# Attention of a hybrid block: q loaded once and copied up by ScalarE, both halves of a head in turn

## The chip, the cores and the metric

The kernel runs on one core of a Trainium2 chip. The metric is device time in microseconds of one execution; the times shown are three runs. The profile is of one further execution, taken by the hardware profiler. Engines are named as in the profile: PE (matrix multiply) with PEld (its weight loads), DVE (VectorE), ACT (ScalarE), POOL (GpSimd) and SP (SyncE, which issues all the DMAs here).

## The reference

One transformer block over 1024 tokens of width 1024 in float32. From the normed input come a gated delta-rule branch (4 heads of 128, in chunks of 64 tokens: the state chain) and an attention branch (8 heads of 64). Their outputs go through the output projection, a residual and a gated feed-forward layer (width 2816). The change touches the attention branch:

```python
DILATED_PATTERNS = ((128, 1), (512, 4), (2048, 16))
def dilated_attention(q, k, v, rel_bias):
    ...
    parts = [dilated_band(qh, kh, vh, rel_bias, win, dil) for win, dil in DILATED_PATTERNS]
    ...
    wts = jnp.exp(ms - jnp.max(ms, axis=0, keepdims=True))
    out = jnp.sum(wts[..., None] * nums, axis=0) / jnp.sum(wts * ss, axis=0)[..., None]
```

Each query sees the last 128 tokens, every 4th of the last 512 and every 16th of the last 2048, with a bias by distance and head, and the three parts share one softmax. A key that several patterns reach counts as often as they reach it.

## The kernel before

**Who sets the order.** The kernel is written as many Python generators ("strands"), each of which yields one operation or waits for an event or a buffer. While the program is built, `Weaver.run` picks the next operation by estimated start times (`Op.__init__` has a cost for each operation, `LAG` the delays between engines, and DMAs have an estimated landing) and by the strand's priority (a small number goes first). The result is one fixed order for each engine's queue; on the chip each engine goes through its own and waits on semaphores. The state chain has priority 0, loads 3, attention 5, the projections (`main`) and the output projection (`out_proj`) 9: on PE these last two fill what the others leave. All operations are recorded at one line, L273, so the views go by tile names.

**The stage.** From about 270 us on, four things share the engines: the last projections of the input (`pj`; in the order bq1, bk1, bq2, bk2, bq3, bk3 and then the gates, `ORDER`, line 48), the state chain (tiles `p`, `state`, `R`, `vn`, `o`), attention, and from about 500 us on the output projection (`pw`), which needs attention's results.

**Attention.** Keys and queries of a projection are stored to DRAM by `proj_qk` in two halves of 512 tokens, each as a high and a low part (`d_q`, `d_k`; `ev_q2[m][b]` and `ev_k2[m][b]` fire when half b of the pair of heads m is stored). Work goes by groups (z, hd): half z of the tokens of head hd. `a_order` (line 1446) lists the 16 groups: the first half of heads 0 to 3, the second of heads 0 and 1, the first of heads 4 to 7, then the second of heads 2 to 7. For each group in this order

- `head_loads` (line 1449) waits for both halves of q and k of its pair of heads, then issues the loads: `qs0` and `qs1` (q high and low, each loaded twice, to partitions 0 to 63 and 64 to 127), `ks` (k high on the lower and low on the upper partitions, 512 tokens for z = 0 and 1024 for z = 1) and `strip` (the biases). These tiles have two buffers each, so one group is loaded ahead;
- `head_prep` (line 1472) adds the parts to `qf` on DVE or POOL, whichever the planner finds earlier;
- `value_loads` (line 1480) loads values twice: `vn` (near keys, by classes of tokens, four DMAs of 32 partitions, 4 or 5 slots of 128) and `vf` (far keys, one or two blocks of four);
- `unit` (line 1499) is one tile of 128 queries, four for each group: score matmuls into `pS`, of `qs` against near keys and of `qf`, in four rows of 32, against far keys (the first tile of z = 0 has no far keys); bias and minimum on DVE (`Sr`, `mx`), exponential on ACT, transposes on PE (`tp`), and splits into high and low parts on ACT and DVE (`ptn`, `ptf`);
- `values` (line 1571) multiplies them by the values into `pV`, 12 matmuls for z = 0 and 18 for z = 1, adds the parts on ACT and DVE (`plow`, `ptmp`) and stores to `d_mix`.

`attention` (line 1607) starts a unit when at most FLY = 6 others are under way.

**Behind it.** `mix_load` (line 1694) loads token tile t of the result when all eight heads have finished half t // 4 of the tokens, so `out_proj` can begin its first tile when the first half is done for every head. Loading the weights of the output projection (`load_wo`: `wor`, `woh`, `wol`) starts after the state chain. The loads of the feed-forward weights (`wraw`) start when attention is done.

Of the kernel before, what the change touches and what calls it, by code (L numbers as in the profile page):

```python
# [11 lines left out]
F32 = mybir.dt.float32  # L12
F32R = mybir.dt.float32r
# [8 lines left out]
P = 128  # L22
S = 1024
# [4 lines left out]
AH = 8  # L28
# [13 lines left out]
TAIL = 5  # L42
ATT = 700.0
EARLY = 4
PWO = (2, 3, 2)
SWITCH = 120.0
BREATH = 200.0
# [3 lines left out]
def sub(ap, dims, off=0):  # L51
    return bass.AP(tensor=ap.tensor, offset=ap.offset + off, ap=[list(d) for d in dims])
# [475 lines left out]
def block_kernel(ctx: ExitStack, tc: tile.TileContext, a, out):  # L528
# [888 lines left out]
    def chain_out(o, t):  # L1417
# [14 lines left out]
        for c in range(2):  # L1432
# [10 lines left out]
    ev_lv = {key: Event() for key in ev_ld}  # L1443
    ev_att = [[Event() for _ in range(4)] for _ in range(AH)]

    a_order = [(0, 0), (0, 1), (0, 2), (0, 3), (1, 0), (1, 1), (0, 4), (0, 5), (0, 6), (0, 7),
               (1, 2), (1, 3), (1, 4), (1, 5), (1, 6), (1, 7)]

    def head_loads():
        for z, hd in a_order:  # L1450
            n = 512 * (z + 1)
            c0 = S - n
            m, e = hd // 2, hd % 2
            r0 = hd * 64
            for b in range(2):
                yield ev_q2[m][b]
                yield ev_k2[m][b]

            qs = []
            for i in range(2):  # L1460
                z_ = yield at.get([P, 512], F32R, name="qs%d" % i)
                for x in (0, 64):
                    yield SY.dma_start(z_[x:x + 64, :].bitcast(F32), d_q[m, i, 64 * e:64 * e + 64, c0:c0 + 512])
                qs.append(z_)
            ks = yield at.get([P, S], F32R, name="ks")
            for i in range(2):
                yield SY.dma_start(ks[64 * i:64 * i + 64, 0:n].bitcast(F32), d_k[i, r0:r0 + 64, 0:n])
            strip = yield at.get([P, 576], F32, name="strip")
            yield SY.dma_start(strip[:], d_bias[hd])
            w.spawn(head_prep(z, hd, qs, ks, strip, c0), 3)  # L1470

    def head_prep(z, hd, qs, ks, strip, c0):

        qf = yield at.get([P, 512], F32, name="qf")
        yield After(*[q[:] for q in qs])
        yield Either(*[x.tensor_tensor(qf[:], qs[0][:].bitcast(F32), qs[1][:].bitcast(F32), ALU.add) for x in (V, G)])
        cur[z, hd] = qs, qf, ks, strip, c0
        ev_ld[z, hd].fire()

    def value_loads():  # L1480
        for z, hd in a_order:
            for t in range(4 * z + 4):
                yield ev_v[hd // 4][t]

            k0 = 1 - z
            v = yield at.get([P, 5, P], F32R, name="vn")
            x = AH * P
            for r in range(4):
                yield SY.dma_start(v[32 * r:32 * r + 32, k0:, :].bitcast(F32),
                                   sub(d_v[:], [[4 * x, 32], [P * x, 5 - k0], [1, P]], hd * P + (3 * z * P + r) * x))  # L1490
            vf = []
            for b in range(z + 1):
                y = yield at.get([P, 4, P], F32R, name="vf", bufs=3)
                vf.append(y)
                yield SY.dma_start(y[:].bitcast(F32), sub(d_v[:], [[4 * x, P], [x, 4], [1, P]], hd * P + 512 * b * x))
            vals[z, hd] = v, vf
            ev_lv[z, hd].fire()

    def unit(z, hd, I, group):
# [34 lines left out]
        banks.put(ps)  # L1534
        n_sc[z, hd] = n_sc.get((z, hd), 0) + 1
        if n_sc[z, hd] == 4:
            at.put(*qs, qf, ks, strip)
        if len(parts) == 2:
            yield V.tensor_tensor(mx[:, 0:1], mx[:, 0:1], mx[:, 1:2], ALU.min)
        yield A.activation(Sr[:, 0:W], Sr[:, 0:W], AF.Exp, scale=-1.0, bias=mx[:, 0:1],  # L1540
# [29 lines left out]

    def values(z, hd, pts):
        yield ev_lv[z, hd]
        v, vf = vals[z, hd]
        m, e = hd // 2, hd % 2
        pn, far = pts
        yield After(pn[:], *[x[:] for x in far])
# [1 line left out]
        for h in range(2):  # L1578

            po = yield banks.get([P, 2, 4, 2, 32], F32, name="pV")  # L1580
            ops = []
            for k in (1, 3, 2, 4) + ((0,) if z else ()):
                i, n = (max(k - 1, 0), 2 if 0 < k < 4 else 1)
                ops.append((po[:, :, i:i + n].rearrange("p c i r j -> p c i (r j)"), v[:, k, :],
                            pn[:, :, max(2 * k - 1, 0):min(2 * k + 1, 8), 64 * h:64 * h + 64]))
            for k, f in enumerate(far):
                i = int(k == z)
                for r in range(2):
                    ops.append((po[:, :, i:, r, :], vf[k][:, 3 - 2 * h - r, :], f[:, :, 2 * h + r, i:, :]))
            yield [mm(o, l, r, n == 0, n == len(ops) - 1) for n, (o, l, r) in enumerate(ops)]  # L1590
            if not h:
                tmp = yield at.get([64, 512], F32, name="ptmp")
            low = yield at.get([64, 4, 2, 32], F32, name="plow", bufs=1)
            yield A.copy(low[:], po[0:64, 1])
            yield V.tensor_tensor(low[:], po[0:64, 0], low[:], ALU.add)

            tt = sub(tmp[:], [list(tmp[:].ap[0]), [P, 4], [-1, 2], [-4, 32]], 127 - 2 * h)
            yield V.tensor_tensor(tt, po[64:128, 0], low[:], ALU.add)
            banks.put(po)
            at.put(low)  # L1600
        at.put(v, *vf, pn, *far)
        yield SY.dma_start(d_mix[4 + m, 64 * e:64 * e + 64, z * 512:(z + 1) * 512], tmp[:])
        at.put(tmp)
        for g_ in range(2):
# [787 lines left out]
```

## Time and profile before

| | |
|---|---|
| three runs | 1271.48, 1273.46, 1274.88 us (median 1273.46) |
| the profiled execution | 1270.66 us, span 1268.9 us |
| mean granted PE clock | 0.997 |
| DMA bytes, mean rate | 216.40 MB, 171 GB/s over the span |
| attention: first and last score matmul | 290.4 and 528.7 us |
| attention: last value matmul | 550.5 us |

In the prediction, a row of a table of stretches has the start and end in us, the length, then for PE, PEld, DVE, ACT and POOL the busy time with the number of instructions, then PE's granted clock, the share of time in which the DMA engines were busy, and GB/s (fewer columns where the view is of one tile). A row of waits reads: engine and what waited, after the arrow what ended the wait, then the sum in us, the number of times, and the longest. A row of the chain has start, length and what it was; "DMA ks<-d_k" there is the time from issue to landing. A row of groups has the count, busy us, the mean ns of one, and the idle time ahead of it with what ended it. A row of DMA issues has the count and the KB of each.

### The profile page before, as it was taken

The numbers are of one execution on the slowest core, as the hardware profiler recorded it, in microseconds if no ns is written. First come the engines' busy times: TensorE is split into PE (matmuls) and PEld (weight loads), VectorE is DVE, ScalarE is ACT, GpSimd is POOL, SyncE is SP. The second block draws the span as 40 slices with busy tenths as digits, with TensorE's granted clock in tenths as the row PEclk, the third lists the DMA queues.
The fourth block names the chain that finished last, engine by engine and source line by source line (L and its number), as shares of the span: only waits on it lengthen the run. The fifth ranks groups of instructions, "written<-read, shape, count | busy, mean of one in ns | idle before, by whom it ended". The sixth has DMA issues, their size and how long they took to land.

```text
span 1268.9 us, 20103 instructions
## 1 busy us (share of the span) xinstructions
PE 1242.0 (98%) x6989; PEld 1026.7 (81%) x6989; DVE 974.3 (77%) x1913; ACT 562.9 (44%) x1162; POOL 180.1 (14%) x153
## 2 busy tenths in 40 slices
PE   8999999999999999999999999999999999999997
PEld 7888798788888787788788888888888887888886
DVE  5689969738988777867798878776677766975886
ACT  7544521136655556545554333333333334534541
POOL 1133411102221110100111101110001100000111
PEclk9999999999999999999999999999999999999999
DMA  8626463779985789667533543223333138734335
GB/s 281 209 73 181 147 206 104 143 228 288 280 232 179 216 251 260 203 217 231 191 125 119 167 155 108 86 77 104 125 125 102 42 106 311 253 128 151 97 124 199
DMA packets 177317, 216.40 MB, mean 171 GB/s; under 512 B 38032, under 2 KB 93712, under 8 KB 177216
## 3 DMA queue, kind: packets, MB, share of 16 engines
q1 hardware_dynamic: 177216, 215.12, 54.2%
q8 instruction: 56, 0.92, 0.3%
q14 instruction: 45, 0.37, 0.1%
HBM read 152.90 MB, written 64.52 MB: 171 GB/s over the span
## 4 chain that ended last, share of the span: by engine, by line
PE 60%; DVE 4%; DMA 4%; SPq 1%; issue 1%; ACT 1%; POOL 0%; DVEq 0%; POOLq 0%; ACTq 0%
PE bank L273 46%; PE pw L273 6%; PE pj L273 2%; PE tp L273 2%; PE p L273 1%; PE pV L273 1%; PE pS L273 1%; SPq L273 1%; DMA da<-d_hid 1%; DMA h2l<-d_h 1%; DMA wor<-in_w_out 1%; PE rp L273 1%; DMA ks<-d_k 0%; DMA qs<-d_q 0%; DVE x L273 0%
## 5 line engine op out<-in xcount | busy, mean ns | idle before, releaser
L273 PE MATMUL pj<-hTh,w 128*128 128x512 f32 x768 | 263.3, 402 | 5.6 <-ACT hTh L273 5.6
L273 PEld LDWEIGHTS pj<-hTh,w 128*128 128x128 f32 x768 | 145.5, 189 | 37.6 <-ACT hTh L273 5.6
L273 ACT CAST wbh<-wraw 128x512 fp32r<-128x512 f32 x130 | 80.2, 621 | 200.6 <-PE bank L273 129.0
L273 PE MATMUL pj<-hTl,w 128*128 128x512 f32 x384 | 151.0, 393 | 0.0
L273 DVE TENSOR_TENSOR wbl<-wraw,wbh 128x512 fp32r<-128x512 f32 x131 | 93.6, 717 | 30.0 <-ACT wbh L273 29.9
L273 PE MATMUL bank<-views 128*128 128x512 f32 (+1 forms) x307 | 85.6, 387 | 0.6 <-ACT views L273 0.6
L273 PEld LDWEIGHTS pj<-hTl,w 128*128 128x128 f32 x384 | 72.9, 190 | 12.4 <-DVE hTl L273 0.5
L273 PE MATMUL bank<-views,dah 128*128 128x512 f32 (+1 forms) x214 | 74.4, 384 | 0.0
L273 PE MATMUL bank<-dbh,views 128*128 128x512 f32 (+1 forms) x201 | 71.0, 383 | 0.0
L273 PEld LDWEIGHTS bank<-views 128*128 128x128 f32 x307 | 57.4, 188 | 13.1 <-ACT views L273 1.0
L273 POOL TENSOR_TENSOR m<-m,m 128x512 f32<-128x512 f32 x18 | 28.4, 1579 | 254.0 <-DVE r L273 168.6
L273 PE MATMUL pw<-woh,mh 128*128 128x512 f32 x128 | 51.9, 406 | 0.0
L273 PE MATMUL pw<-woh,ml 128*128 128x512 f32 x128 | 50.2, 392 | 0.0
L273 PE MATMUL pw<-wol,mh 128*128 128x512 f32 x128 | 50.1, 392 | 0.0
L273 PE MATMUL bank<-dbh,dah 128*128 128x512 f32 (+1 forms) x129 | 49.7, 386 | 0.0
L273 DVE SCALAR_TENSOR_TENSOR yc<-raw,convw,yc 128x1024 f32<-128x1024 f32 x36 | 47.1, 1308 | 0.3
L273 ACT CAST w<-wr 128x512 fp32r<-128x512 f32 x53 | 32.5, 619 | 32.7 <-PE pj L273 25.7
L273 ACT ACTIVATE Sr<-Sr,mx 128x512 f32<-128x512 f32 (+2 forms) x64 | 39.9, 624 | 15.5 <-DVE mx L273 15.0
L273 PEld LDWEIGHTS bank<-views,dah 128*128 128x128 f32 x214 | 39.9, 188 | 8.3
L273 DVE TENSOR_TENSOR m<-bank,m 128x512 f32<-128x512 f32 x44 | 30.1, 685 | 19.1 <-PE bank L273 19.1
L273 PEld LDWEIGHTS bank<-dbh,views 128*128 128x128 f32 x201 | 37.6, 188 | 8.3
L273 DVE TENSOR_TENSOR w<-wr,w 128x512 fp32r<-128x512 f32 x41 | 31.6, 781 | 15.2 <-ACT w L273 14.9
(387 smaller groups left out, 3288.3 us busy)
## 6 DMA issues: line engine op xcount, KB each, us to landing
wr<-in_w_in SPq DMA_DIRECT2D x56, 256.0 KB
wraw<-in_w_gate SPq DMA_DIRECT2D x52, 256.0 KB
wraw<-in_w_up SPq DMA_DIRECT2D x52, 256.0 KB
views<-d_hid SPq DMA_DIRECT2D x47, 256.0 KB
db<-in_w_down SPq DMA_DIRECT2D x40, 256.0 KB
qs<-d_q SPq DMA_DIRECT2D x64, 128.0 KB
da<-d_hid SPq DMA_DIRECT2D x30, 256.0 KB
vf<-d_v SPq DMA_DIRECT2D x24, 256.0 KB
```

The source lines that it names most:

```text
L273: op.fn(*op.args, **op.kw)
```

## The change

`a_order` takes both halves of heads 0 to 4 in turn, then the first half of heads 6, 7 and 5, then the second half of heads 5, 6 and 7. A group waits for half z of q and k only. q is loaded once, to the lower partitions; two ACT copies in `head_prep` fill the upper ones. For heads 0 to 5 (`once`) the second group keeps the first one's `ks` and `strip` and loads only the upper 512 keys. Values are loaded in blocks of 512 tokens, `vn` like `vf` with four slots and `VB` = 3 buffers each; for heads 0 to 5 the second group keeps the first one's block. The buffers are given back after the second group. `values` reads the same slots from the blocks.

```diff
+VB = 3
...
-    a_order = [(0, 0), (0, 1), (0, 2), (0, 3), (1, 0), (1, 1), (0, 4), (0, 5), (0, 6), (0, 7),
-               (1, 2), (1, 3), (1, 4), (1, 5), (1, 6), (1, 7)]
+    a_order = [(z, hd) for hd in range(5) for z in range(2)] + [(0, 6), (0, 7), (0, 5), (1, 5), (1, 6), (1, 7)]
+
+    once = range(6)
 
     def head_loads():
+        kept = {}
         for z, hd in a_order:
-            n = 512 * (z + 1)
-            c0 = S - n
+            c0 = (1 - z) * 512
             m, e = hd // 2, hd % 2
             r0 = hd * 64
-            for b in range(2):
-                yield ev_q2[m][b]
-                yield ev_k2[m][b]
 
             qs = []
+            yield ev_q2[m][z]
             for i in range(2):
                 z_ = yield at.get([P, 512], F32R, name="qs%d" % i)
-                for x in (0, 64):
-                    yield SY.dma_start(z_[x:x + 64, :].bitcast(F32), d_q[m, i, 64 * e:64 * e + 64, c0:c0 + 512])
+                yield SY.dma_start(z_[0:64, :].bitcast(F32), d_q[m, i, 64 * e:64 * e + 64, c0:c0 + 512])
                 qs.append(z_)
-            ks = yield at.get([P, S], F32R, name="ks")
+            yield ev_k2[m][z]
+            more = hd in kept
+            ks, strip = kept.pop(hd) if more else (None, None)
+            if not more:
+                ks = yield at.get([P, S], F32R, name="ks")
+            x, y = 512 if more else 0, 512 * z + 512
             for i in range(2):
-                yield SY.dma_start(ks[64 * i:64 * i + 64, 0:n].bitcast(F32), d_k[i, r0:r0 + 64, 0:n])
-            strip = yield at.get([P, 576], F32, name="strip")
-            yield SY.dma_start(strip[:], d_bias[hd])
+                yield SY.dma_start(ks[64 * i:64 * i + 64, x:y].bitcast(F32), d_k[i, r0:r0 + 64, x:y])
+            if not more:
+                strip = yield at.get([P, 576], F32, name="strip")
+                yield SY.dma_start(strip[:], d_bias[hd])
+                if hd in once:
+                    kept[hd] = ks, strip
             w.spawn(head_prep(z, hd, qs, ks, strip, c0), 3)
 
     def head_prep(z, hd, qs, ks, strip, c0):
+        for q in qs:
+            yield After(q[:])
+            yield A.copy(q[64:128, :], q[0:64, :])
 
         qf = yield at.get([P, 512], F32, name="qf")
-        yield After(*[q[:] for q in qs])
...
     def value_loads():
+        x = AH * P
         for z, hd in a_order:
-            for t in range(4 * z + 4):
-                yield ev_v[hd // 4][t]
-
-            k0 = 1 - z
-            v = yield at.get([P, 5, P], F32R, name="vn")
-            x = AH * P
-            for r in range(4):
-                yield SY.dma_start(v[32 * r:32 * r + 32, k0:, :].bitcast(F32),
-                                   sub(d_v[:], [[4 * x, 32], [P * x, 5 - k0], [1, P]], hd * P + (3 * z * P + r) * x))
-            vf = []
-            for b in range(z + 1):
-                y = yield at.get([P, 4, P], F32R, name="vf", bufs=3)
-                vf.append(y)
-                yield SY.dma_start(y[:].bitcast(F32), sub(d_v[:], [[4 * x, P], [x, 4], [1, P]], hd * P + 512 * b * x))
-            vals[z, hd] = v, vf
+            vals[z, hd] = vals.get((0, hd), [])[:1] if hd in once else []
+            for b in range(len(vals[z, hd]), z + 1):
+                for t in range(4 * b, 4 * b + 4):
+                    yield ev_v[hd // 4][t]
+
+                v = yield at.get([P, 4, P], F32R, name="vn", bufs=VB)
+                for r in range(4):
+                    yield SY.dma_start(v[32 * r:32 * r + 32].bitcast(F32),
+                                       sub(d_v[:], [[4 * x, 32], [P * x, 4], [1, P]], hd * P + (4 * b * P + r) * x))
+                vf = yield at.get([P, 4, P], F32R, name="vf", bufs=VB)
+                yield SY.dma_start(vf[:].bitcast(F32), sub(d_v[:], [[4 * x, P], [x, 4], [1, P]], hd * P + 512 * b * x))
+                vals[z, hd].append((v, vf))
             ev_lv[z, hd].fire()
...
-            at.put(*qs, qf, ks, strip)
+            at.put(*qs, qf, *(() if z == 0 and hd in once else (ks, strip)))
...
-                ops.append((po[:, :, i:i + n].rearrange("p c i r j -> p c i (r j)"), v[:, k, :],
+                ops.append((po[:, :, i:i + n].rearrange("p c i r j -> p c i (r j)"), blocks[z if k else 0][0][:, (k - 1) % 4, :],
...
-        at.put(v, *vf, pn, *far)
+        at.put(pn, *far)
+        if z or hd not in once:
+            for x in blocks:
+                at.put(*x)
```

More of the change, by code (lines that the diff above doesn't have):

```diff
@@ L1572, in values @@
         yield ev_lv[z, hd]
-        v, vf = vals[z, hd]
+        blocks = vals[z, hd]
         m, e = hd // 2, hd % 2
@@ L1588, in values @@
                 for r in range(2):
-                    ops.append((po[:, :, i:, r, :], vf[k][:, 3 - 2 * h - r, :], f[:, :, 2 * h + r, i:, :]))
+                    ops.append((po[:, :, i:, r, :], blocks[k][1][:, 3 - 2 * h - r, :], f[:, :, 2 * h + r, i:, :]))
             yield [mm(o, l, r, n == 0, n == len(ops) - 1) for n, (o, l, r) in enumerate(ops)]
```

## The prediction

> **What bounds the kernel now.** I read the page first, then the table of stretches over the part that the change touches (268 to 640 us), then the waits, the chain and the queue inside it. The page's head says which engine matters:
>
> ```profile
> span 1268.9 us, 20103 instructions
> PE 1242.0 (98%) x6989; PEld 1026.7 (81%) x6989; DVE 974.3 (77%) x1913; ACT 562.9 (44%) x1162; POOL 180.1 (14%) x153
> ```
>
> PE is busy for 98% of the span. The edit takes no matrix multiply away and adds none (see the value blocks below), so it can only give back or lose PE's idle time and PE's slow clock. How much of that lies in its reach, by stretch (start and end, length, then busy us of each engine with its instructions in brackets, PE's granted clock, DMA share, GB/s):
>
> ```profile
> 268.00:360.00 92.00, 89.27 (x678) 75.12 (x676) 74.36 (x233) 52.12 (x146) 18.84 (x19) 1.00 0.91 272
> 360.00:404.00 44.00, 42.83 (x324) 37.05 (x324) 37.84 (x113) 26.77 (x81) 10.51 (x9) 1.00 0.62 188
> 404.00:432.00 28.00, 24.66 (x197) 20.47 (x196) 19.79 (x76) 13.82 (x44) 3.67 (x3) 0.94 0.89 256
> 268.00:640.00 372.00, 361.31 (x2486) 299.63 (x2485) 291.41 (x799) 211.50 (x551) 58.77 (x59) 1.00 0.76 230
> ```
>
> PE idles 372.00 - 361.31 = 10.69 us in the whole part. One stretch is out of line: 404 to 432 loses 28.00 - 24.66 = 3.34 us, and its clock is 0.94, another 0.06 x 28 = 1.7 us. No gain far above 10.69 + 1.7 = 12.4 us can come out of this part. Why that stretch stalls is in three views: PE's and VectorE's waits in it, the chain, and SyncE's queue.
>
> ```profile
> PE pS L273 <- DMA ks<-d_k: 3.3, 2, 2.3
> ```
> ```profile
> DVE qf L273 <- DMA qs<-d_q: 5.5, 3, 4.4
> ```
> ```profile
> 415.24 6.25 DMA ks<-d_k
> ...
> 421.69 0.48 PE pS L273 x2
> ```
> ```profile
> 360.01 2.41 SPq L273 DMA_DIRECT2D qs<-d_q  x4
> ...
> 380.07 0.34 SPq L273 DMA_DIRECT2D d_k<-bh  x1
> ...
> 403.13 0.39 SPq L273 DMA_DIRECT2D d_k<-bh  x1
> ...
> 404.85 2.42 SPq L273 DMA_DIRECT2D qs<-d_q  x4
> ```
>
> The scores (pS) wait for keys that SyncE had issued by 415.24 and that landed 6.25 us later. Between 362.4 and 404.85 SyncE issued no q at all: the ninth group of the list, (0, 6), may not load before both halves of the last key projection are stored (403.13), and the list is served in order. Then the loads of several groups go out in a burst. The scores themselves show the hole (length, PE's busy time on pS, count in brackets, clock, DMA):
>
> ```profile
> 268.00:390.00 122.00, 22.46 (x272) 1.00 0.86 258
> 390.00:410.00 20.00, 0.00 (x0) 1.00 0.58 165
> 410.00:430.00 20.00, 6.69 (x84) 0.91 0.94 263
> ```
> ```profile
> L273 PE MATMUL pS<-ks,qs x128: 222/282/454, 290.7 to 527.8; 128*128 128x256 f32 x112, 128*128 128x128 f32 x16
> L273 PE MATMUL pV<-ptf,vf x96: 252/278/336, 305.9 to 550.5; 128*128 128x192 f32 x64, 128*128 128x256 f32 x32
> L273 PE MATMUL pj<-hTh,w x768: 387/389/793, 5.6 to 503.3; 128*128 128x512 f32 x192
> ```
>
> A first-half group has 32 recorded score matmuls and a second-half group 40 (a unit has two on q, and eight on qf where it has far keys), 576 in all. The 272 up to 390 are exactly the first eight groups (6 x 32 + 2 x 40); then none is left to do. PE bridges 390 to 410 with projections (pj), so the hole costs nothing there; it costs where attention restarts.
>
> **The change part by part.** *Order and gates.* The new list has ten groups (heads 0 to 4, both halves: 5 x 32 + 5 x 40 = 360 matmuls) ahead of head 6. At the pace before the hole, 272 in the 99 us from 290.7 to 390, or 2.7 per us, they last until 291 + 133 = 424; and (0, 6) now waits only for the first half of its projections, whose keys were stored at 380.07 instead of 403.13. Attention then takes PE time that the projections have here from 390 to 410, so that store comes later than 380, but 40 us are there for it. I take the hole as gone. What is late next is the ordinary idling around it: (2.73 + 1.17) us in the 136 us up to 404, so 0.8 in 28. The stretch gives 3.34 - 0.8 = 2.5 us of idling and 1.7 us of clock: **-4.2 us**. The ends: 0, if the restart only moves, and -5.0, if the stretch becomes free of gaps.
>
> *Fewer transfers.* From the page's list of DMA issues:
>
> ```profile
> qs<-d_q SPq DMA_DIRECT2D x64, 128.0 KB
> vf<-d_v SPq DMA_DIRECT2D x24, 256.0 KB
> strip<-d_bias SPq DMA_DIRECT2D x16, 288.0 KB
> ks<-d_k SPq DMA_DIRECT2D x16, 256.0 KB
> vn<-d_v SPq DMA_DIRECT2D x32, 80.0 KB
> ks<-d_k SPq DMA_DIRECT2D x16, 128.0 KB
> vn<-d_v SPq DMA_DIRECT2D x32, 64.0 KB
> ```
>
> These are 200 issues and 29,696 KB. After: qs 32; ks 28 of 128 KB and 4 of 256; strip 10; vf 18; vn 72 of 64 KB (blocks of four instead of strips of four or five): 164 issues and 20,800 KB. SyncE's queue is spared 36 issues, some 22 us at 2.42/4 each, and the DMA engines 30% of attention's bytes. Beside a busy PE that is worth nothing; it pays where a load is waited for. Such places are two waits of PE in the first stretch,
>
> ```profile
> PE pS L273 <- DMA d_k<-bh: 0.9, 1, 0.9
> PE pS L273 <- DMA ks<-d_k: 0.8, 1, 0.8
> ```
>
> and the gaps after q of (1, 6), which goes out behind the weights of the output projection (one row of the chain, then 10-us stretches):
>
> ```profile
> 475.60 5.41 DMA qs<-d_q
> ```
> ```profile
> 480.00:490.00 10.00, 9.64 (x56) 7.99 (x54) 8.74 (x17) 8.01 (x14) 1.29 (x1) 1.00 1.11 242
> 490.00:500.00 10.00, 8.90 (x72) 6.72 (x73) 7.87 (x28) 6.31 (x18) 0.00 (x0) 1.00 0.93 302
> ```
>
> I take half of each: **-0.8** of 1.7 and **-0.7** of 0.36 + 1.10. The ends are none and all.
>
> *An earlier end of attention.* The 304 scores after the hole took the 117 us from 411 to 528, 2.6 per us; at that pace, without the hole, 576 last 221 us and end near 512 instead of 528. The loads of the feed-forward weights start only when attention is done, and the stage behind them is short of VectorE time (18.98 of 20 us):
>
> ```profile
> 555.46 1.39 SPq L273 DMA_DIRECT2D wraw<-in_w_gate  x1
> ```
> ```profile
> 620.00:640.00 20.00, 18.55 (x86) 14.96 (x85) 18.98 (x32) 12.90 (x26) 4.93 (x4) 1.00 0.63 210
> ```
>
> Loads some 15 us sooner spread that preparation; of its 1.45 us of PE gaps I take **-0.5** (ends 0 and -1.45).
>
> *The copies.* 2 x 16 = 32 new copies of 64x512 on ScalarE, from the lower to the upper partitions. The trace has no such copy. The nearest rows:
>
> ```profile
> L273 ACT CAST bh<-bl 128x512 fp32r<-128x512 f32 x10 | 6.2, 621 | 13.8 <-DVE bl L273 11.2 <-POOL w L273 1.0 <-POOL state L273 0.8
> L273 ACT COPY vn<-p 64x512 f32<-64x512 f32 x15 | 8.7, 579 | 2.0 <-PE p L273 1.8
> ```
> ```profile
> L273 DVE TENSOR_TENSOR ptmp<-pV,plow 64x256 f32<-64x256 f32 x32 | 20.3, 636 | 1.0
> L273 DVE TENSOR_TENSOR plow<-pV,plow 64x256 f32<-64x256 f32 x32 | 13.2, 411 | 8.8 <-ACT plow L273 8.6
> ```
>
> As a plain copy 0.58 to 0.62 us. The only row with a move across the halves is VectorE's ptmp, which also reverses and strides: 636/411 = 1.55 times plow, so at most 0.96. I take 0.62, the row that also reads and writes SBUF: 32 x 0.62 = 19.8 us of ScalarE (ends 18.5 and 31). ScalarE is busy 211.5 of the 372 us, so there is room. The cover of the 1.24 us that they add to a group's load is the prefetch of one group, 32/2.7 = 12 us of scores. With the cover gone, and at the rate that the second rival works out, 10 us would reach PE. PE's waits on ScalarE are tenths of a us today; the only one of 360 to 404 is
>
> ```profile
> PE p L273 <- ACT vn L273: 0.2, 1, 0.2
> ```
>
> A tenth more work on ScalarE makes little of that; I take **+0.7** (ends 0 and +10).
>
> *The value blocks.* 8 x 12 + 8 x 18 = 240 value matmuls as before, with three buffers of each kind of block. A second-half group's new block waits until the group before it has given one back, a group ahead of its use: I take nothing; without that cover it costs one block's load, five issues or 3 us of queue, in part beside other PE work.
>
> Sum: -4.2 - 0.8 - 0.7 - 0.5 + 0.7 = **-5.5 us**. The profiled execution took 1270.66 us around its span of 1268.9, so it would take 1265.2. The median of the three runs shown, 1273.46, lies 2.8 above it; its counterpart is 1268.0.
>
> **The rivals.** *The room closes again* (chance 0.22). PE is busy for 97% of this part, its order is planned by estimates, and a new list moves every gap. Then the 404 stretch's loss comes back at another restart, the copies eat the small gains, and the time is 1273 (1270 to 1277). Against it: the hole has a cause that the new list takes away.
>
> *ScalarE becomes the gate* (0.19, slower). Today only VectorE or GpSimd stands still when q is late. After the edit ScalarE's queue holds a copy that waits for the DMA, and behind it stand the state chain's vn and o, the exponentials and the splits of ptn and ptf, which PE waits for. The price: in the stall above VectorE's longest wait of 4.4 us came with a PE wait of 2.3, a rate of 0.52. The waits for q in the whole part are
>
> ```profile
>   DMA qs<-d_q: 9.5, 7
> ```
>
> If these 9.5 us and the copies' 19.8 reach PE at that rate, it is 0.52 x 29.3 = +15.2; with the gains of 6.2 left, +9.0: 1282. It decides from a rate of 6.2/29.3 = 0.21 upwards. For it: landing times were missed by microseconds at 415. Against it: 30% of the bytes go. The Trainium skill says in "TensorE: Matmul & The Clock Gate", section "Architectural detail: the array is 16× 32×32, not 1× 128×128", that ScalarE and VectorE take their work strictly first in, first out. By that rule a late q stops all of ScalarE for the whole wait, which is this rival; the trace of before has such a wait on VectorE and, since ScalarE reads no q there, cannot show one on ScalarE.
>
> *The output projection starves* (0.07, slower). Its first attention tile needs the first half of all heads, and head 5's is now the 13th group of 16 instead of the eighth. Its 456th score comes at 291 + 456/2.7 or /2.6, 460 to 466, and its values some 23 us later (527.8 to 550.5 at the end of attention): by 489, ahead of 503.3, where the projections run out. With attention 15% slower it comes at 515, and PE, left with little but attention, loses most of 12 us: 1281 with the other terms as forecast less the restart's gain.
>
> **How the numbers follow.** Forecast 0.52, no change 0.22, ScalarE 0.19, starvation 0.07. A difference under 0.3% (3.8 us: 1269.6 to 1277.3) can't be told from none. The forecast's own range is 1264 (every gain at its full end, -9.6) to 1271 (half of the restart and little else); 0.06 of its 0.52 lies above 1269.6, and 0.02 of the second case below: faster 0.48, same 0.06 + 0.20 = 0.26, slower 0.19 + 0.07 = 0.26. The range goes from 1262, all of the 12 us, to 1281 and leaves out the upper halves of the two slow cases, 0.13, and little else.
>
> **What would show it.** Right: no 20 us without pS between 291 and the end of attention, clock 1.00 from 400 to 440, the last value matmul near 535, the first wraw near 540, copies of 0.6 us with ScalarE waiting less than 5 us for q. Wrong: waits of several us of ScalarE for q with PE waiting for vn, ptn or ptf behind them; a gap between the last pj and the first pw; a 3 us stall at another restart.

## The result, and the profile after

The changed kernel takes 1278.39 us (median of 10 runs, 1276.87 to 1283.94) where the kernel before takes 1272.24 beside it (10 runs, 1270.55 to 1275.72): a ratio of 1.0053 (95%: 1.0036 to 1.0071), 6 us slower. The forecast was 5.5 us faster. The profiled execution of the changed kernel took 1283.94 us, the longest of the ten; 2.6 us of its delay are there before attention starts, where the two kernels are the same. It is not a typical run: its mean granted clock was 0.994, and five of the ten had 0.997. What follows therefore goes by stretches, not by the span. Line numbers of the changed kernel are one higher (L274).

The page's head:

```profile
span 1282.2 us, 20077 instructions
PE 1251.6 (98%) x6989; PEld 1027.8 (80%) x6989; DVE 978.3 (76%) x1925; ACT 571.6 (45%) x1180; POOL 176.2 (14%) x151
```

PE's busy time grew by 9.6 us with the same 6989 matrix multiplies: part of the loss sits in multiplies that ran slowly, not in gaps. The table of stretches of the changed kernel, columns as before:

```profile
268.00:360.00 92.00, 88.81 (x681) 73.56 (x680) 71.22 (x218) 56.47 (x150) 15.09 (x16) 1.00 0.75 230
360.00:404.00 44.00, 42.20 (x338) 34.28 (x337) 39.28 (x126) 29.57 (x84) 11.29 (x10) 1.00 0.72 207
404.00:432.00 28.00, 26.86 (x227) 22.63 (x226) 25.17 (x82) 20.50 (x60) 7.96 (x7) 1.00 0.69 203
470.00:500.00 30.00, 26.83 (x190) 21.01 (x189) 20.04 (x61) 14.06 (x44) 1.27 (x1) 0.89 0.65 193
530.00:560.00 30.00, 26.28 (x140) 19.08 (x138) 14.13 (x26) 11.00 (x21) 1.12 (x2) 0.94 0.75 236
268.00:640.00 372.00, 358.30 (x2458) 291.26 (x2458) 282.04 (x787) 211.76 (x552) 49.31 (x53) 0.99 0.66 201
```

The old stall is gone, as forecast: 404 to 432 idles 1.14 us instead of 3.34, at clock 1.00 instead of 0.94. Two new ones stand in its place: 470 to 500 idles 3.17 us at 0.89, and 530 to 560 idles 3.72 us at 0.94. In the kernel before the same two stretches are these:

```profile
470.00:500.00 30.00, 28.54 (x186) 22.74 (x187) 20.01 (x54) 17.25 (x39) 1.29 (x1) 1.00 1.03 287
530.00:560.00 30.00, 29.48 (x186) 24.78 (x185) 20.84 (x53) 14.26 (x37) 1.91 (x3) 1.00 0.44 139
```

From the two tables, idle time changes by -2.2 at the old stall and by +1.7 and +3.2 at the new ones. The clock returns 0.06 x 28 = 1.7 us and takes 0.11 x 30 + 0.06 x 30 = 5.1.

That is not the whole difference of this pair of executions, which lie 13.3 us apart. To see the rest, the same work has to be compared, and not the same stretch of time: from the last multiply ahead of this stage (tile `pm`) to the first of the feed-forward layer (tile `bank`). The kernel before, the changed kernel, and further down `e5_gains_later`, which has neither stall:

```profile
267.40:621.10 353.70, 344.47 (x2410) 286.06 (x2408) 273.11 (x768) 199.58 (x527) 53.84 (x55) 1.00 0.77 232
270.00:636.00 366.00, 352.30 (x2408) 286.18 (x2409) 278.11 (x781) 209.07 (x546) 49.31 (x53) 0.99 0.66 199
268.10:623.60 355.50, 347.76 (x2410) 283.34 (x2408) 277.80 (x781) 208.38 (x545) 49.78 (x53) 1.00 0.67 204
```

For the same multiplies the changed kernel takes 366.0 - 353.7 = 12.3 us more here. Idle time is 13.70 - 9.23 = 4.5 of it. PE's busy time is 7.8, of which the clock explains 5.1 - 1.7 = 3.4. The other 4.4 us are a third share: multiplies that take longer, as the profile counts them, at full clock. The transposes (`tp`, 256 in each) alone went from 37.18 to 39.14 us. This share is in neither stall, and in `e5_gains_later` it is still there (347.76 busy against 344.47, with no half clock to explain it). Why the new order makes them longer was not taken apart and stays open.

**Stall 1, at 483.** One row of the chain, then ScalarE's and PE's timelines (start, length, engine, operation; in square brackets the idle time ahead and what ended it):

```profile
474.89 8.34 DMA qs<-d_q
```
```profile
483.25 1.25 ACT L274 CAST qs<-qs 64x512 fp32r<-64x512 f32 x2 [3.78 <-DMA qs<-d_q]
484.52 0.37 ACT L274 COPY plow<-pV 64x256 f32<-64x256 f32 x1
484.79 0.72 ACT L274 ACTIVATE Sr<-Sr,mx 128x512 f32<-128x512 f32 x1
```
```profile
485.73 1.19 PE L274 MATMUL pS<-ks,qs 128*128 128x256 f32 x4 [3.17 <-ACT Sr L274]
```

The last group's q is issued at 474.89, behind 3 MB of weights of the output projection that SyncE issued from 468.48 to 472.43, and needs 8.34 us to land. The copy waits for it at the head of ScalarE's queue for 3.78 us. Behind the copy stand the part sum `plow` and the exponential `Sr` of other tiles, whose data were ready, and PE's next scores wait for `Sr`.

**Stall 2, at 541 to 547.** SyncE's queue, and PE's waits from 503 to 560 (sum, times, longest):

```profile
524.30 0.49 SPq L274 DMA_DIRECT2D d_mix<-ptmp  x1
524.88 1.97 SPq L274 DMA_DIRECT2D wor<-in_w_out  x4
526.91 0.42 SPq L274 DMA_DIRECT2D gpost<-in_g_mix_post  x1
527.38 0.42 SPq L274 DMA_DIRECT2D gpre<-in_g_ffn_pre  x1
528.90 1.57 SPq L274 DMA_DIRECT2D d_gt<-gst  x2
536.33 0.37 SPq L274 DMA_DIRECT2D mx<-d_mix  x1
```
```profile
PE pw L274 <- ACT mh L274: 3.6, 2, 2.9
```

Attention is done at 524.30, when its last store (`d_mix`) goes out. The queue is served in order, so only behind it does SyncE issue 1 MB of weights (`wor`) and 1 MB of gains. Then it stores the last two gates (`d_gt`, 256 KB each) and issues nothing more until the first of these has landed, 7.41 us after its issue. Only then does it load attention's result for the output projection (`mx`, split into `mh`). That load doesn't read the gates; it needs their buffer. The kernel gives `mx` the same two slots that hold the last two gates (`mxS` and `gstS[1, 1]` are both `rawS.slots[:2]`), so each of the two first `mx` waits for one of the stores. A buffer of its own for `mx` was not tried. The kernel before has the same hold in its queue:

```profile
507.20 1.12 SPq L273 DMA_DIRECT2D d_gt<-gst  x2
514.16 1.08 SPq L273 DMA_DIRECT2D mx<-d_mix  x2
```

There PE had attention to do until 550.5. In the changed kernel it has none left, and the input projections have run out too:

```profile
L274 PE MATMUL pV<-ptf,vf x96: 248/277/402, 313.5 to 522.5; 128*128 128x192 f32 x64, 128*128 128x256 f32 x32
L274 PE MATMUL pj<-hTh,w x768: 387/389/796, 5.8 to 526.5; 128*128 128x512 f32 x192
L274 PE MATMUL pw<-woh,mh x128: 387/389/794, 526.7 to 635.3; 128*128 128x512 f32 x128
```

Attention ends 28 us earlier than before, but `pj`, which attention displaced, ends 23 us later (503.3 before). The two end together.

**What a stall costs beyond itself.** Stretches of 2 us behind stall 1:

```profile
484.00:486.00 2.00, 0.28 (x1) 0.31 (x2) 1.02 (x3) 1.60 (x5) 1.27 (x1) 0.82 0.64 165
486.00:488.00 2.00, 2.00 (x20) 1.22 (x19) 0.43 (x3) 1.30 (x3) 0.00 (x0) 0.50 0.73 201
488.00:490.00 2.00, 2.00 (x8) 1.44 (x5) 1.59 (x7) 0.78 (x3) 0.00 (x0) 0.50 0.81 250
490.00:492.00 2.00, 2.00 (x9) 1.72 (x8) 1.17 (x3) 0.63 (x3) 0.00 (x0) 0.50 0.04 14
492.00:494.00 2.00, 2.00 (x15) 1.87 (x15) 1.48 (x3) 0.37 (x1) 0.00 (x0) 0.98 0.00 0
```

After the wait of 3.17 us PE runs at half clock for some 6.5 us: another 3 us are lost in time that counts as busy.

### The profile page after: what moved, and what is told of

The parts are those of the page before. It is cut to its first block, busy times and chain, and to the rows that moved or that the text cites. A ratio compares the mean times of both kernels' runs of the same rounds, so it can differ in the third digit from the quotient of the medians.

```text
span 1282.2 us, 20077 instructions
## 1 busy us (share of the span) xinstructions
PE 1251.6 (98%) x6989; PEld 1027.8 (80%) x6989; DVE 978.3 (76%) x1925; ACT 571.6 (45%) x1180; POOL 176.2 (14%) x151
## 4 chain that ended last, share of the span: by engine, by line
PE 74%; DVE 11%; DMA 8%; ACT 2%; issue 2%; SPq 1%; POOL 1%; DVEq 0%; POOLq 0%; ACTq 0%
PE bank L274 46%; PE pj L274 13%; PE pw L274 5%; PE tp L274 4%; PE pS L274 2%; PE p L274 2%; DVE yc L274 2%; DMA qs<-d_q 1%; PE pV L274 1%; PE pm L274 1%; SPq L274 1%; DMA ks<-d_k 1%; PE rp L274 1%; DMA wr<-in_w_in 1%; DVE Sr L274 1%
## 5 line engine op out<-in xcount | busy, mean ns | idle before, releaser
L274 PE MATMUL pj<-hTh,w 128*128 128x512 f32 x768 | 267.4, 406 | 6.4 <-ACT hTh L274 5.8
L274 PEld LDWEIGHTS pj<-hTh,w 128*128 128x128 f32 x768 | 146.3, 190 | 42.3 <-issue 6.8
L274 ACT CAST wbh<-wraw 128x512 fp32r<-128x512 f32 x131 | 81.1, 621 | 203.0 <-PE bank L274 132.8
L274 PE MATMUL pj<-hTl,w 128*128 128x512 f32 x384 | 151.9, 396 | 0.0
L274 DVE TENSOR_TENSOR wbl<-wraw,wbh 128x512 fp32r<-128x512 f32 x131 | 92.7, 709 | 31.2 <-ACT wbh L274 31.1
L274 PE MATMUL bank<-views 128*128 128x512 f32 (+1 forms) x307 | 85.5, 386 | 0.0
L274 PEld LDWEIGHTS pj<-hTl,w 128*128 128x128 f32 x384 | 73.5, 191 | 12.4 <-DVE hTl L274 0.7
L274 PE MATMUL bank<-views,dah 128*128 128x512 f32 (+1 forms) x214 | 74.4, 384 | 0.0
L274 PE MATMUL bank<-dbh,views 128*128 128x512 f32 (+1 forms) x201 | 71.0, 383 | 0.0
L274 PEld LDWEIGHTS bank<-views 128*128 128x128 f32 x307 | 57.5, 188 | 12.2
L274 POOL TENSOR_TENSOR m<-m,m 128x512 f32<-128x512 f32 x18 | 28.4, 1580 | 253.8 <-DVE r L274 155.0
L274 PE MATMUL pw<-woh,mh 128*128 128x512 f32 x128 | 52.5, 410 | 3.6 <-ACT mh L274 3.6
L274 PE MATMUL pw<-woh,ml 128*128 128x512 f32 x128 | 50.6, 395 | 0.1
L274 PE MATMUL pw<-wol,mh 128*128 128x512 f32 x128 | 50.4, 393 | 0.0
L274 PE MATMUL bank<-dbh,dah 128*128 128x512 f32 (+1 forms) x129 | 49.7, 386 | 0.0
L274 DVE TENSOR_TENSOR w<-wr,w 128x512 fp32r<-128x512 f32 x42 | 29.6, 711 | 24.1 <-ACT w L274 23.8
L274 ACT ACTIVATE Sr<-Sr,mx 128x512 f32<-128x512 f32 (+2 forms) x64 | 40.0, 625 | 17.2 <-DVE mx L274 16.8
L274 ACT CAST w<-wr 128x512 fp32r<-128x512 f32 x52 | 31.9, 619 | 34.9 <-PE pj L274 25.4
L274 DVE SCALAR_TENSOR_TENSOR yc<-raw,convw,yc 128x1024 f32<-128x1024 f32 x36 | 47.1, 1307 | 0.3
L274 PEld LDWEIGHTS bank<-views,dah 128*128 128x128 f32 x214 | 39.9, 188 | 8.3
L274 DVE TENSOR_TENSOR m<-bank,m 128x512 f32<-128x512 f32 x44 | 30.2, 686 | 19.1 <-PE bank L274 19.1
L274 PEld LDWEIGHTS bank<-dbh,views 128*128 128x128 f32 x201 | 37.6, 188 | 8.3
```

The lines of the kernel that those rows point to most:

```text
L274: op.fn(*op.args, **op.kw)
```

## The experiments

Each ratio is against runs of the kernel before on the same chip, with its 95% interval. "Two stalls" is the theory that the loss is these two and nothing else; the main rival is that a new list only moves gaps about, so that any small edit would shift the time as much. One profiled execution stands for each kernel.

### The parts by themselves

**One load of q and the copies, nothing else** (`e2_copies`), on the kernel before:

```diff
-                for x in (0, 64):
-                    yield SY.dma_start(z_[x:x + 64, :].bitcast(F32), d_q[...])
+                yield SY.dma_start(z_[0:64, :].bitcast(F32), d_q[...])
...
+        for q in qs:
+            yield After(q[:])
+            yield A.copy(q[64:128, :], q[0:64, :])
...
```

> The kernel before with q loaded once and copied up by ScalarE, and nothing else: the old list of groups, the old gates, no sharing. Theory A: the copies are hidden, 1270 to 1275, against 1272 before. Theory B: ScalarE waits for q by several us at the burst near 411 and behind the weights near 475, PE behind it, and the time is 1276 to 1280.

Measured: 1272.57 us, 0.9992 (0.9981 to 1.0003). The copies as such cost nothing that can be measured. The hole is as it was (no score from 390 to 410), and yet the restart behind it is better than before, 1.83 us of idling at clock 1.00:

```profile
404.00:432.00 28.00, 26.17 (x200) 21.89 (x198) 21.23 (x68) 16.11 (x42) 6.64 (x6) 1.00 0.86 246
```

In the changed kernel the copies take what was assumed, and wait for q ten times, more than the 5 us in all that the prediction allowed (first row count, min/median/max in ns; second row sum, times, longest):

```profile
L274 ACT CAST qs<-qs x32: 610/617/621, 280.9 to 483.9; 64x512 fp32r<-64x512 f32 x32
```
```profile
ACT qs L274 <- DMA qs<-d_q: 13.1, 10, 3.8
```

**Half gates alone** (`e7_half_gates`), on the kernel before:

```diff
-            for b in range(2):
-                yield ev_q2[m][b]
+            yield ev_q2[m][z]
+            for b in range(z + 1):
                 yield ev_k2[m][b]
```

> The kernel before, in which a group waits only for the halves of q and k that it reads; list, loads and copies stay. (0, 6) and (0, 7) may then load some 20 us sooner. If the hole of scores from 390 to 410 and the stall behind it were worth what I forecast: PE idles under 1.5 us from 404 to 432, its clock stays 1.00 there, and the time is 1268 to 1270 against 1272.5. If a stall that is taken away here comes back behind it: 1271 to 1275.

Measured: 1279.02 us, 1.0058 (1.0035 to 1.0081): slower, against the expectation. Its stretch of the old stall:

```profile
404.00:432.00 28.00, 23.33 (x184) 18.47 (x183) 23.80 (x76) 15.44 (x46) 5.26 (x5) 0.94 0.74 206
```

The gate that the prediction named as the hole's cause is gone, and so is the hole (49 scores from 390 to 410), but the stretch idles 4.67 us instead of 3.34, at the same clock. Opening the gate was not enough. PE also idles 4.70 us from 268 to 360 (2.73 before) and 3.10 from 470 to 500 (1.46 before); where the whole 0.6% comes from was not taken apart.

**New list and half gates, q still loaded twice, nothing shared** (`e1_order`): the edit above and the changed kernel's `a_order`.

> The kernel before with the new list of groups and the half gates alone: q is loaded twice as before, nothing is copied by ScalarE, nothing is shared between the halves of a head. Theory A (the order costs: attention has ended when the projections run out, and nothing is left to cover the wait for the first tiles of the output projection): the gap between the last pj and the second tile of pw is there, with 3 us or more of PE idling near 540, and the time is 1276 to 1280. Theory B (the copies cost, through ScalarE's queue): without copies the loss is gone, 1269 to 1273.

Measured: 1275.18 us, 1.0022 (1.0010 to 1.0034). 404 to 432 idles 2.86 us, so the list takes little of the idling. Its clock there is 1.00, but that says little of the list: `e10_before_gains` below, with the old list, idles 4.23 us there at 1.00 as well. Idling at 470 to 500 is 2.38 us, and 530 to 560 is full:

```profile
404.00:432.00 28.00, 25.14 (x196) 20.39 (x194) 23.10 (x70) 17.21 (x51) 4.38 (x4) 1.00 0.85 229
...
470.00:500.00 30.00, 27.62 (x199) 21.89 (x199) 18.98 (x57) 13.43 (x43) 0.00 (x0) 1.00 0.85 236
...
530.00:560.00 30.00, 30.00 (x162) 24.02 (x160) 17.48 (x33) 14.84 (x31) 2.60 (x4) 1.00 0.68 219
```

So the gap near 540 that the first of the two expectations forecast isn't there, although attention ends as early as in the changed kernel (last value multiply 519.5, last `pj` 520.9). The difference is in SyncE's queue: the weights and gains go out from 512.75 to 515.99, ahead of attention's last store at 521.03; the gates' store follows at 522.50 and `mx` at 524.55, 2.05 us later. An early end of attention is thus not enough for stall 2; the bulk loads must also stand just ahead of the gates' store. (This execution was the fastest of its nine, 1271.16 us.)

**Copies and half gates on the old list** (`e12_copies_half`): the edits of the first two together.

> The kernel before with q loaded once and copied by ScalarE, and with the half gates; whole strips of values and the old list. The half gates alone gave 1.0058, the copies alone 0.9992, both with the values in blocks 0.9977. If the one load of q is what the half gates lacked (DMA queue free at the restart): 0.998 to 1.000, 404 to 432 with 26 us or more of PE. If the value blocks made it: about 1.005, with PE waits of several us for mx, ks and ptmp from 380 to 500. If neither, and each list moves its gaps by itself: anything between, with a stall at another place.

Measured: 1274.26 us, 1.0011 (0.9999 to 1.0023), between the two answers expected and nearer the first: with q loaded once, the half gates lose some 0.5% less than alone. 404 to 432 is good, and the loss sits at 470 to 500, where ScalarE again waits for a late q:

```profile
404.00:432.00 28.00, 26.57 (x210) 22.69 (x210) 27.07 (x89) 19.33 (x56) 6.00 (x6) 1.00 0.80 219
...
470.00:500.00 30.00, 26.35 (x161) 20.43 (x161) 14.70 (x42) 15.14 (x38) 1.29 (x1) 0.83 0.89 254
```
```profile
483.26 0.62 ACT L273 CAST qs<-qs 64x512 fp32r<-64x512 f32 x1 [4.25 <-DMA qs<-d_q]
```

So stall 1 doesn't need the new list; it comes on the old one as well where a copy waits for a late q.

**The changed kernel with the old list and nothing shared** (`e8_old_list`): copies, half gates and value blocks stay.

```diff
-    a_order = [(z, hd) for hd in range(5) for z in range(2)] + [...]
-    once = range(6)
+    a_order = [(0, 0), (0, 1), (0, 2), (0, 3), (1, 0), (1, 1), ...]
+    once = ()
```

> The changed kernel with the list of groups of before and nothing shared between the halves of a head (the old list has no room for that): half gates, one load of q, copies and blocks of values stay. If the new list carries the loss: 1270 to 1274. If the copies or the blocks of values carry it: 1276 to 1280.

Measured: 1267.65 us, 0.9977 (0.9966 to 0.9989), faster than the kernel before.

```profile
404.00:432.00 28.00, 27.31 (x237) 22.60 (x236) 25.72 (x90) 18.58 (x53) 5.06 (x5) 1.00 0.90 244
...
470.00:500.00 30.00, 29.08 (x189) 23.57 (x192) 22.71 (x58) 18.86 (x45) 4.24 (x3) 1.00 0.85 217
```

Its attention runs until 539.0 and its `pj` until 505.3, so the cover of before is there, and PE is full from 500 to 560. What the changed kernel loses against this one comes with the list and the sharing. Against `e12_copies_half` it has the value blocks in addition, and it issues a group's q before it waits for the keys; the 0.3% between them are theirs, or the new plan's that came with them. That stays open.

### The two stalls

**q of the last group ahead of the weights** (`e3_q_first`), on the changed kernel:

```diff
     def load_wo():
+        yield ev_lastq
...
+            if (z, hd) == a_order[-1]:
+                ev_lastq.fire()
```

> The changed kernel, but the loads of the output projection's weights start only when the q of the last group has been issued. This takes away what the last q queued behind (8.3 us from issue to landing). Theory B: ScalarE's wait of 3.8 us and PE's 3.2 us at 485 go, with the clock that they cost, and the time is 1272 to 1275 against 1278.4. Theory A: that stall goes, but the gap near 541 stays or grows, because the weights come later: 1275 to 1280.

Measured: 1275.69 us, 1.0015 (1.0006 to 1.0025). Stall 1 is gone, stall 2 stays:

```profile
470.00:500.00 30.00, 29.01 (x216) 23.51 (x215) 22.25 (x67) 15.72 (x47) 1.30 (x1) 1.00 0.73 215
...
530.00:560.00 30.00, 26.23 (x130) 19.92 (x129) 18.97 (x36) 13.72 (x27) 2.60 (x4) 0.94 0.70 223
```

**Feed-forward weights later** (`e4_ff_later`). In the changed kernel a split of feed-forward weights (`wbh`) stands just ahead of `mh` in ScalarE's queue. Is that what PE waits for?

```diff
     def load_gu():
+        for e in ev_mix[1]:
+            yield e
```

> The changed kernel, but the loads of the feed-forward weights start only when the second token tile of the output projection is prepared. Their splits then no longer stand in ScalarE's queue ahead of that tile's. If the gap near 541 comes from this queueing (the split waited for a weight that landed 6.3 us after issue): the gap of 3.6 us shrinks to under 1 us and the time is 1273 to 1276. If it comes from the missing cover (no attention left, projections done, the gates still on their way to DRAM and back): the gap stays at 2 us or more and the time is 1277 to 1280.

Measured: 1282.13 us, 1.0073 (1.0061 to 1.0085). The splits now stand behind `mh`, and the stretch is no better:

```profile
530.00:560.00 30.00, 25.34 (x125) 18.91 (x123) 14.27 (x25) 10.35 (x20) 2.48 (x3) 0.94 0.69 218
```

PE's wait for `mh` falls from 2.87 to 1.76 us, but a wait of 1.77 us for `ml`, its low part on VectorE, comes in its place. The split took part in the wait, then, but moving it gains nothing; the gates' store still holds SyncE for 7.1 us (528.67 to 535.77). The loads of the feed-forward weights themselves went out hardly sooner or later than in the changed kernel (from 538.30 instead of 538.86). Stall 1 cost more in this execution (25.65 us busy from 470 to 500), so the ratio isn't the price of the edit.

**Gains behind the gates, too** (`e5_gains_later`): `e3_q_first` and

```diff
         ev_x3.fire()
+        yield ev_gt
         for nm, key in (("gpost", "g_mix_post"), ("gpre", "g_ffn_pre")):
```

> The kernel of e3 (last q ahead of the weights), and the two gain vectors, 1 MB that SyncE issues just ahead of the last gates' store, are loaded behind that store. If the gap near the second tile of pw (PE idle 3.6 us in e3 between 530 and 545, clock 0.94) comes from the gates' store lying behind 2 MB of loads: the store lands some 3 us sooner, the gap falls to under 1.5 us, and the time is 1271 to 1274, against 1275.7 for e3. If the store's delay is not what the tile waits for: the gap stays above 2.5 us and the time is 1275 to 1277.

Measured: 1270.93 us, 0.9996 (0.9981 to 1.0010), with 470 to 500 at 29.07 and

```profile
530.00:560.00 30.00, 29.65 (x157) 23.01 (x156) 19.35 (x35) 15.30 (x32) 2.22 (x4) 1.00 0.76 240
```

**The gains alone** (`e9_gains_only`), on the changed kernel, q behind the weights as it was:

> The changed kernel, in which only the loads of the two gains (1 MB) go behind the gates' way through DRAM (d_gt) in SyncE's order; the weights' burst ahead of the last group's q stays. Two-stall theory: the gap of pw near 541 to 547 goes, the stall near 480 to 485 stays (ScalarE waits 3 to 4 us for q); of 1.0053 the 0.0019 that separated the two kernels before goes: 1.0034, 1276.3 us. Rival, one cause (the late q alone delays all that follows, so that the gap comes with it): the gap stays, 1.005. Second rival, the plan only moves its gaps: any ratio from 0.997 to 1.007, with a stall at a place of its own.

Measured: 1274.46 us, 1.0013 (1.0000 to 1.0026). SyncE's queue, then the two stretches (500 to 530 is full):

```profile
522.91 0.85 SPq L274 DMA_DIRECT2D d_gt<-gst  x2
523.81 0.45 SPq L274 DMA_DIRECT2D gpost<-in_g_mix_post  x1
524.31 0.45 SPq L274 DMA_DIRECT2D gpre<-in_g_ffn_pre  x1
525.13 0.38 SPq L274 DMA_DIRECT2D mx<-d_mix  x1
```
```profile
470.00:500.00 30.00, 26.83 (x200) 21.34 (x201) 19.78 (x62) 14.08 (x44) 1.65 (x2) 1.00 0.72 198
530.00:560.00 30.00, 29.60 (x158) 23.39 (x157) 19.46 (x35) 15.33 (x31) 2.21 (x4) 1.00 0.75 242
```

With the 1 MB of gains behind it, the gates' store holds SyncE for 2.2 us (522.91 to 525.13) instead of 7.4, and stall 2 is gone while stall 1 stays: the two are separate. The output projection's first to last `pw`, 108.6 us in the changed kernel, takes 102.8 here:

```profile
L274 PE MATMUL pw<-woh,mh x128: 387/389/500, 520.6 to 623.4; 128*128 128x512 f32 x128
```

One stall alone leaves 1.0015 or 1.0013, none 0.9996, both 1.0053. Stall by stall the ratio falls by 0.17 and 0.19% when the other is already gone, and by 0.38 and 0.40% when it is not; with intervals of 0.10 to 0.18% on each ratio, whether the two add up or make each other worse stays open. The theory that the loss is these two and nothing else does not hold: without them the kernel is level with the one before, and not faster as forecast, and the third share above, some 4 us, is still in it.

**The same move in the kernel before** (`e10_before_gains`):

> The kernel before with the same move of the two gains. Two-stall theory: there the last groups of attention cover the gates' way through DRAM, so nothing is gained: ratio 0.9985 to 1.0015, the stretch 530 to 560 full as before. Rival, the move is a gain of its own: 0.998 or less, and then the run with it said little of the change.

Measured: 1273.81 us, 1.0010 (0.9996 to 1.0024), with 530 to 560 full. No gain where attention covers the store, so the move mends a harm that the change did.

### Attention kept as cover

**The last group waits until six gates are projected** (`e6_hold_last`), on `e3_q_first`:

```diff
+            if len(gates) == 6:
+                ev_six.fire()
...
         for z, hd in a_order:
+            if (z, hd) == (1, 7):
+                yield ev_six
```

> The kernel of e3, and the units of the last group (1, 7) start only when six of the eight gate projections are through. Its loads stay where they are. This gives PE attention work back between the last projection and the second tile of pw. If the gap there is a missing cover: the last value matmul moves from 513 to 530 or later, PE idles under 1.5 us between 530 and 545, and the time is 1271 to 1274, against 1275.7 for e3. If the end of attention decides instead (what starts behind it comes later): 1275 to 1279.

Measured: 1267.88 us, 0.9968 (0.9956 to 0.9980): the lowest ratio here (the interval of `e8_old_list` overlaps it), with

```profile
268.00:640.00 372.00, 366.31 (x2500) 300.13 (x2499) 298.09 (x808) 228.86 (x581) 61.63 (x61) 1.00 0.67 206
```

But not by the mechanism expected: attention ended at 517.3, not at 530 or later. Its weights and gains are issued from 506.18 to 509.04, the gates' store follows 9 us later, at 518.08, and the result is loaded at 520.16. That fits the absence of stall 2; it doesn't say why it beats `e5_gains_later`, which has neither stall. From the last `pm` to the first `bank` PE idles 5.45 us and is busy for 346.15, against 7.74 and 347.76 there; why was not taken apart.

**The same hold in the kernel before** (`e11_before_hold`):

> The kernel before, in which the units of the last group wait until six gates are projected. Theory that attention was the cover that the change took away: here attention ends at 550, after the gates, and the last group starts when six gates are nearly done anyway, so little moves: 0.9985 to 1.0015. Rival, the hold is good in any kernel (it spreads attention beside the projections): 0.997, as in the changed kernel, which then owes its 0.9968 to the hold and not to the change.

Measured: 1272.59 us, 1.0003 (0.9988 to 1.0017). There the hold is worth nothing.

## Why the prediction was wrong

Three steps of the prediction failed: what attention's end was taken to bring, what was taken to cover the copies, and the premise that PE's busy time stays as it is. The first two are shown by experiments; of the third only the size is known.

- **An earlier end of attention (-0.5) failed.** The end came even earlier than forecast (522.5 against 535; the first `wraw` at 538.86 against 540), and it was booked as a gain without asking what attention was covering. It covered the hold of SyncE's queue by the gates' store, visible before at 507.20 to 514.16. The displaced `pj` then ended with attention instead of 47 us ahead of it, and PE was left with one token tile of `pw`. `e9_gains_only` takes this stall away and gains 0.40%, some 5 us; `e10_before_gains` gains nothing. The early end alone doesn't do it, as `e1_order` shows: there the bulk loads had gone out earlier.
- **The copies (+0.7): their cover failed.** They took 0.617 us each against 0.62 taken, and lost nothing by themselves (0.9992). But the cover that was named, the prefetch of one group, did not hold for the last group, whose q was queued behind 3 MB of weights: PE lost 3.17 us there, and more by the clock. `e3_q_first` takes this stall away and gains 0.38%.
- **The premise failed** that the edit can only give back or lose PE's idle time and its slow clock, because the multiplies are the same. They are, but at full clock they took 4.4 us longer, and the sum had no term for it.
- **Order and gates (-4.2)**: the gain came where it was looked for, 2.2 us of idling and 1.7 of clock. The reason was only half right. `e2_copies`, with the old list, the old gates and the hole, already has 26.17 us busy in 404 to 432, against 25.14 for the new list with q loaded twice and 23.33 for half gates alone. The burst of loads after the hole counted for at least as much as the hole. The clock's part is chance to some degree: the old list ran this stretch at 1.00, too, in `e10_before_gains`.
- **Fewer transfers (-0.8 and -0.7)**: neither came as time. PE's waits for `ks` up to 480 fell from 4.2 us to 0.3, but others took their place (`ptmp` 1.4, `o` 0.7, `ckd` 0.9), and 268 to 360 went from 89.27 busy us to 88.81. At the weights' burst the sign was wrong: fewer bytes do not help a q that is queued behind 3 MB of other loads, and its wait had moved to ScalarE.
- **The value blocks (0)**: no harm seen; `e8_old_list` leaves open that they helped.
- **The clock** was counted for the old stall and for none that might come: in the profiled execution half clock cost 3.4 us at the first new stall and 1.7 at the second.

Of the rivals, *ScalarE becomes the gate* named the mechanism of stall 1, but not its extent. The rate was 3.17/3.78 = 0.84 at this place, above the 0.52 assumed; beside the other nine waits, 9.3 us together, all of PE's waits on ScalarE up to 480 sum to 1.5 us, so that 3 to 5 us of idling came instead of 15. The rule of the Trainium skill in "TensorE: Matmul & The Clock Gate", section "Architectural detail: the array is 16× 32×32, not 1× 128×128", that ScalarE takes its work strictly first in, first out, agrees with ScalarE's timeline above: `plow` and `Sr` follow the late copy at once. *The output projection starves* was right that PE would run short there, for another reason and a tile later: between the last `pj` and the first `pw` there is no gap (526.5 to 526.7), and head 5's place in the list did no harm. *The room closes again* is true as a sum: the restart's 3.9 us came, and more was lost at other places. That any small edit shifts the time as much is not excluded: the two controls on the kernel before stayed at 1.0003 and 1.0010, but the half gates alone moved it by 0.6%. For the two stalls it is answered all the same, since each went when the load named as its cause was moved, and the other stayed.

## What to carry to other kernels

Before an activity is made to end earlier, list the waits that it covers today, in the DMA queues too, and ask what else can cover them; work that it displaces ends later. An operation that waits for a DMA belongs on an engine whose queue holds nothing that the busiest engine needs soon, or its load ahead of any bulk transfer. A large load can often be issued behind a small store that a later load waits for; here that was worth 0.2 to 0.4% where the wait was bare, and nothing where it was covered. Ask, too, whether the later load waits for the data or only for the buffer. And the same multiplies in a new order need not keep the busiest engine for the same time.

## What the hardware showed beyond that

- Idle times of 2 to 3 us can halve PE's clock, and need not. It fell to 0.50 for 3.41 us after idle times of 2.25 (kernel before, at 422), 2.00 (`e7_half_gates`), 2.85 (`e3_q_first`) and 2.87 us (stall 2; `pw` took 0.63 to 0.79 us each there, later 0.39), for 6.83 us after 3.17 (stall 1) and for 10.24 us after 2.57 (`e12_copies_half`). The idle time of 2.84 us in `e9_gains_only` was followed by no loss, and `e10_before_gains` ran at half clock twice, for 3.41 us each, without any idle time of 2 us in this part. The Trainium skill, "TensorE: Matmul & The Clock Gate", section "What's actually happening", has the clock at half after at least one idle window of about 3.4 us that runs freely, and full again after as long a busy one; the lengths at half clock, one, two and three times 3.41 us, agree, but idle times well under 3.4 us were enough here.
- The ten runs of the changed kernel scatter partly with it: the five at a mean clock of 0.997 took 1276.87 to 1278.57 us, the three longest (1282.16 to 1283.94) had 0.993 to 0.995; but one at 0.994 took 1278.86.
- A copy on ScalarE from the lower to the upper 64 partitions takes 617 ns for 64x512, no more than its 621 ns cast of 128x512 that stays on its partitions: the move across the halves costs nothing there.
- A 256 KB store of a gate, issued just behind 2 MB of loads, held the queue for 7.4 us. With half of these loads behind it the next load went out 2.2 us after it, and with all of them issued 6.5 us earlier (`e1_order`) 2.05 us after it.
